# The recurrence of a hybrid encoder layer: its instructions recorded and issued by a list schedule in the kernel, with the branch products moved to other PSUM banks

## The chip, the cores and the metric

The kernel runs on one core of one Trainium2 chip. The metric is the device time of one execution in microseconds (us), the median of the runs shown. Engines are named as in the profile: PE (TensorE matmul), PEld (its weight load), DVE (VectorE), ACT (ScalarE), POOL (GpSimd), SP (the queue that issues most DMAs).

## The reference, cut to what matters

Sequence 512, model width 1024, two layers. Each layer projects the normalized input `h` and runs five mixers on it; their outputs are merged by gates:

```python
for l in range(DEPTH):
    p = jnp.einsum('bsd,dc->bsc', h, w_in[l])
    pa, pb, pc, pd, pm = split_last(p, mixer_sizes)
    o_a = mixer_dilated(pa, table_a)
    o_b = mixer_rwkv(pb, ...)          # a linear recurrence over 512 steps, both directions
    o_c = mixer_axial_gqa(pc, ...)
    o_d = mixer_diff(pd, ...)
    o_m = mixer_memory(pm, mem, w_mem_kv[l])
    y = gated_merge(h, (o_a, o_b, o_c, o_d, o_m), w_branch[l], w_gate[l], b_gate[l])
    out = jnp.einsum('bsd,de->bse', y, w_out[l])
    h = layer_norm(alpha * h + out, ln_g[l], ln_b[l])

# gated_merge, for each mixer i: sigmoid(h @ w_gate_i + b_i) * (o_i @ w_branch_i), summed
```

`mixer_rwkv` has 8 heads of 64; its step is `state = state * w + (state @ a) b^T + v k^T`, `y = state @ r`, run forward and backward and added.

## The kernel before

All activations lie transposed, 128 channels by 512 tokens. A float32 product is made of three matmuls on split operands (`gemm3_steps`, L145): hi*hi (L149), hi*lo (L150), lo*hi (L151), each 128x128 by 128x512. Weights come by DMA in chunks of 128x512 (`wraw`), ACT casts the high part (L135), DVE subtracts for the low part (L136).

Each layer has three stages. First the attention mixers (A, C, D, M). Then the recurrence (mixer B). Then the merge of mixer B (`branch_steps(1, ...)`), the product with `w_out` and the layer norm.

The recurrence works on 4 pairs of heads in 2 directions, 8 units. `early(p, e)` makes what a unit needs (projections `mixed` in the banks `pg`, low-rank products L826, exponentials, the products L907, L92, transposes L941 and L947). `late(p, e)` inverts the 32x32 triangles in 62 dependent DVE steps (L989, L991 on the tile `W`), combines them (L1007, L1014), then for two halves makes L1035, L1050 (read by DVE in L1053), L1061 and the four chained state steps L1068, each of which waits for the copies of the state `ST` on ACT (L1070) and DVE (L1071). `finish(p)` turns the sum of both directions, `SY`, back (L1092) and normalizes it. Many of these matmuls use a part of the array only (64x128, 64x64, 32x32).

The gates and branch products of mixers A, C, D and M (`fill`, L422) depend on nothing in the recurrence. For each of 8 column blocks `branch_steps` makes a gate product of 24 matmuls in a bank, ACT's tanh empties it (L406), then a branch product of 12 matmuls (6 for M), which DVE empties (L412 or L414, then adds to `y` in L416). In `fill` both products use the one bank `pf`:

```python
    ps = ps_f() if ch == "f" else ps_s()      # gate
    ...
    ps = ps_f() if ch == "f" else ps_g()      # branch
```

These are 1,104 matmuls a layer. The code weaves them in by `pull(1)`: after each `yield` of the recurrence one step (three matmuls) of `fill` is emitted; a few steps are pulled in the attention stage already (L649, L728). The final order on each engine is made by the framework's scheduler, which has its own durations; every engine then runs its queue in that order.

Of the kernel before, what the change touches and what calls it, by code (L numbers as in the profile page):

```python
# [13 lines left out]
AF = mybir.ActivationFunctionType  # L14
ALU = mybir.AluOpType
PSUM = bass.MemoryType.PSUM
# [32 lines left out]
NPAR = _off  # L49


@with_exitstack
def encoder_kernel(ctx: ExitStack, tc: tile.TileContext, x, mem, ln_in, rel_bias, w_in, par, w_up, a_up,
                   d_lambda, w_mem, w_branch, w_gate, w_out, lnp, cst, cossin, onehot, cnt, msk, out):
    nc = tc.nc

    const = ctx.enter_context(tc.tile_pool(name="const", bufs=1))
    big = ctx.enter_context(tc.tile_pool(name="big", bufs=1))
# [3 lines left out]
    def ps_g():  # L62
        return pp.tile([128, 512], F32, name="pg", tag="pg", bufs=2)

    def ps_f():
        return pp.tile([128, 512], F32, name="pf", tag="pf", bufs=1)
# [215 lines left out]
    with tc.tile_pool(name="init", bufs=1) as ip:  # L282
# [30 lines left out]
        for t in range(2):  # L313
            for j in range(2):
                ps = ps_s()
# [21 lines left out]
        for i in range(2):  # L337
            ps = ps_m()
# [11 lines left out]
    for l in range(L):  # L350
# [45 lines left out]
        def branch_steps(br, os, nk, done=None, ch="f", pool=wp, gb=1, order=None):  # L396
            k0 = K0[br]
            if os is None:
                os = reload(br, nk)
            for db in range(8):  # L400
                ps = ps_f() if ch == "f" else ps_s()
                w = split_w(w_gate[l, br * 8 + db], 1024, "f")
                yield from gemm3_steps(ps, [(*wk(w, k), hT[:, 0, k, :], hT[:, 1, k, :]) for k in range(8)])
                gt = pool.tile([128, S], F32, name="gt", tag="gt", bufs=gb)
                i = br * 8 + db
                act(gt, ps, AF.Tanh, scale=0.5, bias=hb[:, i:i + 1])  # L406
                ps = ps_f() if ch == "f" else ps_g()
                w = split_w(w_branch[l, db, :, k0 * 128:(k0 + nk) * 128], nk * 128, ch)
                yield from gemm3_steps(ps, [(*wk(w, k), o[:, 0, :], o[:, 1, :]) for k, o in zip(order or range(nk), os)])
                if y[db] is None:  # L410
                    y[db] = big.tile([128, S], F32, name="y", tag="y", bufs=8)
                    stt(y[db], gt, 1.0, ps, ALU.add, ALU.mult)  # L412
                else:
                    stt(gt, gt, 1.0, ps, ALU.add, ALU.mult)  # L414
                    if done is None:
                        tt(y[db], y[db], gt, ALU.add)  # L416
                    else:
                        tt(gt, y[db], gt, ALU.add)
                        done(db, gt)
# [10 lines left out]
        def pull(x):  # L430
            owed[0] += x
            while owed[0] >= 1:
                owed[0] -= 1
                next(fl, None)


        with tc.tile_pool(name=f"att{l}", bufs=1) as at:
# [115 lines left out]
            for hp in range(4):  # L553
# [4 lines left out]
                ps, ps2 = ps_g(), ps_g()  # L558
# [5 lines left out]
                k = k_stack(ps2)  # L564
                q = q_stack(ps)
                ps = ps_g()
# [3 lines left out]
                v = v_pair(vT, 4)  # L570
# [5 lines left out]
                for i in range(2):  # L576
                    b = load_bias(2 * hp + i)
                    p4 = []
                    for qb in range(4):
                        ps = ps_s()  # L580
                        score(ps, q, k, i, qb, S)
                        p, _ = softmax(ps, S, b[:, 384 - 128 * qb:896 - 128 * qb])
# [43 lines left out]
            ps = ps_g()  # L626
# [11 lines left out]
            for b in range(4):  # L638
                q = qn
                g = b // 2  # L640
                of = tile_of("oc", [128, S], F32, 2)
                for i in range(2):
                    p4 = []
                    for qb in range(4):
                        ps = ps_s()
                        score(ps, q, (kh, kl), i, qb, S, g)
                        p, _ = softmax(ps, S)
# [6 lines left out]
                t = gated(of, g2, True)  # L654
# [8 lines left out]
            with tc.tile_pool(name=f"attd{l}", bufs=1) as ad:  # L663
# [12 lines left out]
                for h in range(4):  # L676
                    ps = ps_g()
                    proj(ps, l, 48 + h, hT)
                    k = k_stack(ps)
                    ps = ps_g()  # L680
                    proj(ps, l, 44 + h, hT)
                    q = q_stack(ps)
                    ps = ps_g()
# [3 lines left out]
                    v = v_parts(vT, 4)  # L687
                    b = load_bias(8 + h)
                    p4 = []
                    for qb in range(4):  # L690
                        bs = b[:, 384 - 128 * qb:896 - 128 * qb]
                        ps, ps2 = ps_s(), ps_s()
# [21 lines left out]
            for b in range(2):  # L714
                k = k_stack(kvm[0][:, b, :], 256)
                v = v_pair(kvm[1][:, b, :], 2)
                ps = ps_g()
# [17 lines left out]
        with tc.tile_pool(name=f"rw{l}", bufs=1) as rp:  # L735
# [6 lines left out]
            def recurrence():  # L742
# [341 lines left out]
                def finish(p):  # L1084

                    q = pairs[p]
                    sy, bo = q["sy"], q["bo"]
                    po = ps_o()
                    for c in range(8):
                        for h in range(2):  # L1090
                            rw = slice(64 * (1 - h), 64 * (1 - h) + 64)
                            mm(po[64 * h:64 * h + 64, c * 64:(c + 1) * 64], sy[rw, c, :], ident[rw, rw], start=True, stop=True)  # L1092
                    ys = T("ys", [128, S])
                    nc.scalar.copy(ys, po)
                    yield
                    ps = ps_m()
                    mm(ps, ones_bd, ys, start=True, stop=True)
                    stt(ys, ps, -1.0 / 64, ys, ALU.mult, ALU.add)
                    sq = T("ysq", [128, S])
                    act(sq, ys, AF.Square)  # L1100
                    yield
                    ps = inv_norm(sq, ps_m(), ones_bd, 1.0 / 64, EPSG)
                    yield
                    tt(ys, ys, ps, ALU.mult)
                    ts(ys, ys, P("lng", p), P("lnb", p), ALU.mult, ALU.add)
                    tt(ys, ys, bo, ALU.add)
                    yield
                    g2 = silu2(rp, l, 16 + 14 + p, 1, "ysq")
                    stt(ys, ys, 0.5, g2, ALU.mult, ALU.mult)
                    if p == 3:  # L1110
                        oB.append(finish_o(rp, ys))
                        return
                    hi = rp.tile([128, S], F32R, name="yhi", tag="ysq", bufs=1)
                    nc.scalar.copy(hi, ys)
                    nc.sync.dma_start(out=scr_o[K0[1] + p, :, 0, :], in_=f(hi))
                    lo = ys.bitcast(F32R)
                    tt(lo, ys, f(hi), ALU.subtract)
                    nc.sync.dma_start(out=scr_o[K0[1] + p, :, 1, :], in_=ys)
                    yield

                pairs = {}
                units = [(p, e) for p in range(4) for e in range(2)]
                yield from early(*units[0])
                for n in range(len(units) + 1):
                    live = []
                    if n < len(units):
                        live.append(late(*units[n]))
                    if n and units[n - 1][1] == 1:
                        live.append(finish(units[n - 1][0]))
                    if n + 1 < len(units):  # L1130
                        live.append(early(*units[n + 1]))
                    while live:
                        for g in list(live):
                            if next(g, 0) == 0:
                                live.remove(g)
                            else:
                                yield

            for _ in recurrence():
                pull(1)  # L1140
            for _ in fl:
                pass


        with tc.tile_pool(name=f"out{l}", bufs=1) as op:
# [160 lines left out]
```

## Time and profile before

| | |
|---|---|
| median of 3 runs | 2253.56 us (2253.05 to 2254.36) |
| the profiled execution's own time | 2258.68 us |
| its span, first to last instruction | 2256.9 us |
| PE / PEld / DVE / ACT busy, share of the span | 97% / 75% / 77% / 56% |
| recurrence of layer 0 in the trace | about 515 to 1038 us |
| recurrence of layer 1 in the trace | about 1618 to 2139 us |

The median is 5.1 us below the profiled execution. Matmuls are pipelined and their ends are modelled in the profile, so the busy share of PE says less than the distance from one matmul's start to the next one's.

### The profile page before, as it was taken

Reading aid. Unit: us, or ns where it says so; the run is one execution under the profiler, and the core shown is the slowest. Engines: PE = TensorE matmul, PEld = TensorE weight load, DVE = VectorE, ACT = ScalarE, POOL = GpSimd, SP = SyncE. Lnnn points to the kernel's source line nnn. Section 1 sums busy time; section 2 is a strip of 40 time slices with the busy share of each in tenths; the row PEclk is TensorE's granted clock in tenths of the full one; section 3 lists DMA queues with packets and bytes.
Section 4 is the critical chain, followed back from the end, with each engine's and each line's share of the span. In section 5 each row is a group of like instructions: output and inputs, shape, how many; then the busy total and the mean of one; then the engine's idle time right before and its main releaser. Section 6 shows DMA issues by size and latency. Waiting matters only on the chain.

```text
span 2256.9 us, 36192 instructions
## 1 busy us (share of the span) xinstructions
PE 2191.7 (97%) x13040; PEld 1681.4 (75%) x13040; DVE 1727.2 (77%) x4228; ACT 1272.9 (56%) x2785; POOL 59.2 (3%) x117
## 2 busy tenths in 40 slices
PE   7999999999999999999999999999999999999998
PEld 6777777777777777777787777777777777777776
DVE  7777887677898797975567778766788979879565
ACT  4655666676555555544335656666665646565440
POOL 0000000100000000000000000001000000000000
PEclk9999999999999999999999999999999999999999
DMA  8732133322222321315333322333313213222251
GB/s 285 222 106 80 65 84 107 108 84 89 62 85 67 107 67 61 101 52 188 101 122 104 95 65 70 95 105 93 111 55 99 71 62 100 70 84 69 89 189 38
DMA packets 111780, 220.49 MB, mean 98 GB/s; under 512 B 13240, under 2 KB 23224, under 8 KB 111216
## 3 DMA queue, kind: packets, MB, share of 16 engines
q1 hardware_dynamic: 101456, 195.09, 27.0%
q0 software_dynamic: 10144, 23.08, 3.9%
q8 instruction: 103, 1.69, 0.3%
q14 instruction: 77, 0.63, 0.1%
HBM read 187.66 MB, written 27.31 MB: 95 GB/s over the span
## 4 chain that ended last, share of the span: by engine, by line
PE 72%; DVE 13%; ACT 8%; DMA 4%; issue 3%; SPq 0%; DVEq 0%; ACTq 0%
PE pg L150 10%; PE pg L151 10%; PE pg L149 10%; PE pf L149 6%; PE pf L150 5%; PE pf L151 5%; PE psc L470 4%; PE po L515 3%; PE pt L496 3%; DVE W L991 2%; DVE pr L989 2%; DMA wrawr<-in_w_out_dram 2%; DMA wrawr<-in_w_branch_dram 1%; DVE wlof L136 1%; PE po L505 1%
## 5 line engine op out<-in xcount | busy, mean ns | idle before, releaser
L150 PE MATMUL pg<-hT,whir 128*128 128x512 f32 (+1 forms) x912 | 366.0, 401 | 2.0 <-DVE hT L176 2.0
L149 PE MATMUL pg<-hT,whir 128*128 128x512 f32 (+1 forms) x912 | 364.5, 400 | 3.3 <-ACT whif L135 1.0
L151 PE MATMUL pg<-hT,wlor 128*128 128x512 f32 (+1 forms) x912 | 363.9, 399 | 0.9 <-DVE wlor L136 0.9
L136 DVE TENSOR_TENSOR wlor<-wrawr,whir 128x512 fp32r<-128x512 f32 x240 | 163.8, 687 | 116.0 <-ACT whir L135 105.7
L135 ACT CAST whir<-wrawr 128x512 fp32r<-128x512 f32 x240 | 147.7, 618 | 164.4 <-PE pg L150 113.2
L135 ACT CAST whif<-wrawf 128x512 fp32r<-128x512 f32 (+1 forms) x268 | 162.0, 605 | 126.3 <-PE pf L150 81.9
L149 PE MATMUL pf<-hT,whif 128*128 128x512 f32 x512 | 221.0, 432 | 3.4 <-DVE gt L414 2.9
L136 DVE TENSOR_TENSOR wlof<-wrawf,whif 128x512 fp32r<-128x512 f32 (+1 forms) x268 | 178.6, 668 | 43.1 <-ACT whif L135 37.9
L150 PE MATMUL pf<-hT,whif 128*128 128x512 f32 x512 | 206.7, 404 | 0.0
L151 PE MATMUL pf<-hT,wlof 128*128 128x512 f32 x512 | 205.0, 400 | 0.0
L149 PEld LDWEIGHTS pg<-hT,whir 128*128 128x128 f32 x912 | 172.4, 189 | 41.3 <-ACT whir L135 2.7
L150 PEld LDWEIGHTS pg<-hT,whir 128*128 128x128 f32 x912 | 172.4, 189 | 38.6 <-issue 3.1
L151 PEld LDWEIGHTS pg<-hT,wlor 128*128 128x128 f32 x912 | 172.6, 189 | 37.4 <-DVE wlor L136 3.4
L176 DVE TENSOR_TENSOR pT<-pt,pT 128x512 fp32r<-128x512 f32 x176 | 114.1, 686 | 35.7 <-ACT pT L175 34.6
L175 ACT CAST pT<-pt 128x512 fp32r<-128x512 f32 x176 | 94.6, 588 | 63.6 <-PE pt L496 63.1
L149 PEld LDWEIGHTS pf<-hT,whif 128*128 128x128 f32 x512 | 96.5, 188 | 35.7 <-DVE gt L414 10.3
L496 PE MATMUL pt<-cst,p 128*128 128x128 f32 x704 | 118.2, 273 | 0.0
L151 PEld LDWEIGHTS pf<-hT,wlof 128*128 128x128 f32 x512 | 96.4, 188 | 21.8 <-issue 1.6
L989 DVE TENSOR_TENSOR pr<-W,U 128x60 f32<-128x60 f32 (+24 forms) x496 | 103.3, 208 | 11.4
L991 DVE TENSOR_TENSOR W<-W,pr 128x60 f32<-128x60 f32 (+24 forms) x496 | 102.8, 207 | 11.1
L150 PEld LDWEIGHTS pf<-hT,whif 128*128 128x128 f32 x512 | 96.7, 189 | 19.1 <-issue 4.5
L496 PEld LDWEIGHTS pt<-cst,p 128*128 128x128 f32 x704 | 89.8, 141 | 27.7 <-DVE p L487 2.7
(330 smaller groups left out, 4803.8 us busy)
## 6 DMA issues: line engine op xcount, KB each, us to landing
wrawr<-in_w_in_dram SPq DMA_DIRECT2D x224, 256.0 KB, 2.8
wrawf<-in_w_gate_dram SPq DMA_DIRECT2D x160, 256.0 KB, 2.8
o<-scr_o POOLq DMA_DIRECT2D x26, 512.0 KB, 4.7
wrawf<-in_w_branch_dram SPq DMA_DIRECT2D x48, 256.0 KB, 2.7
bias<-scr_toe SPq DMA_DIRECT2D x24, 448.0 KB, 3.2
scr_o<-os SPq DMA_DIRECT2D x20, 512.0 KB, 2.9
wrawf<-in_w_in_dram SPq DMA_DIRECT2D x32, 256.0 KB, 2.8
wrawr<-in_w_out_dram SPq DMA_DIRECT2D x32, 256.0 KB, 3.1
```

The source lines that it names most:

```text
L135: nc.scalar.copy(hi, raw)
L136: tt(lo, raw, f(hi), ALU.subtract)
L149: mm(ps, ah, bh, start=(i == 0), stop=False)
L150: mm(ps, ah, bl, start=False, stop=False)
L151: mm(ps, al, bh, start=False, stop=(i == n - 1))
L175: nc.scalar.copy(hi, src)
L176: tt(lo, src, f(hi), ALU.subtract)
L470: mm(ps[:, :nk], q[:, i, sl], part[:, i if g is None else g, :nk], start=(j == 0), stop=(j == 1))
L496: nc.tensor.transpose(pt[:, qb * 128:(qb + 1) * 128], p4[qb][:, kb * 128:(kb + 1) * 128], ident)
L515: mm(po, vwin(kb), pT[:, b, :], start=(kb == 0 and b == 0), stop=(kb == nkb - 1 and b == 1))
L989: tt(pr, W[:, t8, s:s + 1].to_broadcast([128, nt, n]), U[:, s:s + 1, rsl].to_broadcast([128, nt, n]), ALU.mult)
L991: tt(W[:, t8, rsl], W[:, t8, rsl], pr, ALU.add)
```

## The change

A class `Conductor` stands between the kernel and the engines. From `record()` on, each engine call is kept with the tiles that it reads and writes, a cost and a rank. The whole rest of `fill` is recorded first, with rank 99; the recurrence then with the number of its unit (late, finish, early within it). `play()` makes a list schedule of both: at each step the engine that can start first takes, among the instructions whose inputs and buffers are ready, the one of the lowest rank (fill's matmuls come last, fill's work on other engines first), and consecutive small matmuls of one unit stay together as a group. The instructions are then issued in that order within `manual_schedule()`, so that each engine keeps it. While recording, a branch product takes a bank `pg`, of which there are two and which the recurrence's projections use as well. No instruction is added or left out.

```diff
+    def add(self, eng, op, real, a, k):
...
+        rank = self.rank
+        if rank[0] == 99 and eng != "tensor":
+            rank = (-1,)
...
+        o["group"] = o["i"]
+        if eng == "tensor":
+            p = self.last.get(self.rank)
+            if p is not None and p["eng"] == "tensor" and p["small"] and o["small"]:
+                o["group"] = p["group"]
...
+    def play(self):
...
+                    t = max(rt[g], s)
+                    o = groups[g][0]
+                    if 0 <= o["rank"][0] < 99 and o["rank"][0] > cur + self.ahead:
+                        continue
+                    pr = o["rank"] + (o["i"],)
+                    win = f0 + self.window(e, o)
...
+                    if t <= win:
+                        if now is None or pr < now[0]:
+                            now = (pr, max(t, f0), g)
+                    elif later is None or (max(t, f0), pr) < (later[1], later[0]):
+                        later = (pr, max(t, f0), g)
+                c = now or later
...
+        with self.tc.manual_schedule():
+            for o in order:
+                o["go"]()
+
+    run, ahead = 0, 1
...
-    nc = tc.nc
+    cd = nc = Conductor(tc)
...
-                ps = ps_f() if ch == "f" else ps_g()
+                ps = ps_f() if ch == "f" and cd.ops is None else ps_g()
...
-            for _ in recurrence():
-                pull(1)
+            cd.record()
+            cd.rank = (99, 0)
             for _ in fl:
                 pass
+            cd.rank = (0, 0)
+            recurrence()
+            cd.play()
```

In the changed kernel every recorded instruction has the line of the recorder (L122), every other one L67, so its rows are told apart by tiles.

PE, the middle of layer 0's recurrence, from a gate product (`pf<-hT`) to the branch product behind it (`pf<-o`); before:

```order
L151 MATMUL pf<-hT,wlof 128x512
L151 MATMUL pg<-hT,wlor 128x512
L149 MATMUL pg<-hT,whir 128x512
L150 MATMUL pg<-hT,whir 128x512
L151 MATMUL pg<-hT,wlor 128x512
L149 MATMUL pg<-hT,whir 128x512
L149 MATMUL pf<-o,whif 128x512
L150 MATMUL pf<-o,whif 128x512
```

The same hand-over in the changed kernel, near the end of layer 0's last unit, where `pt<-ST,PE` is a state step (L1068 of before):

```order
L122 MATMUL pf<-hT,whif 128x512
L122 MATMUL pt<-ST_5493,PE 128x128
L122 MATMUL pf<-hT,whif 128x512
L122 MATMUL pf<-hT,wlof 128x512
L122 MATMUL pt<-ST_5492,PE 128x128
L122 MATMUL pg<-o,whif 128x512 x2
L122 MATMUL pg<-o,wlof 128x512
```

Before, five matmuls of a projection stand between the last gate matmul and the first branch matmul in the same bank; now the branch product stands in another bank and follows one state step later.

PE, the end of layer 0's recurrence, from the last state step on (`po<-cst,SY` is the transpose in `finish` of the last pair); before:

```order
L1068 MATMUL pt<-ST_5131,PE 128x128
L1092 MATMUL po<-cst,SY 64x64
L149 MATMUL pf<-o,whif 128x512
L150 MATMUL pf<-o,whif 128x512
L151 MATMUL pf<-o,wlof 128x512
L149 MATMUL pf<-o,whif 128x512
L150 MATMUL pf<-o,whif 128x512
L151 MATMUL pf<-o,wlof 128x512
L1092 MATMUL po<-cst,SY 64x64 x15
```

The same place in the changed kernel:

```order
L122 MATMUL pg<-o,whif 128x512
L122 MATMUL po<-cst,SY 64x64 x16
L122 MATMUL pg<-o,whif 128x512
L122 MATMUL pg<-o,wlof 128x512
L122 MATMUL pg<-o,whif 128x512 x2
L122 MATMUL pm<-ys,cst 128x512
L122 MATMUL pg<-o,wlof 128x512
L122 MATMUL pf<-hT,whif 128x512 x2
```

Behind the last `po<-cst,SY` stand 30 of the 1,104 matmuls of fill before, and 281 now. Between the recurrence's first low-rank product and that point PE goes from a full-array matmul to a part-array block 97 times before and 80 times now, and back to fill and projection matmuls, from any of the recurrence's other matmuls, 176 times before and 142 times now. On DVE, 82 of fill's weight subtractions (L136) stand ahead of the recurrence's last `SY` before and 62 now, 22 and 14 of its L414, 27 and 14 of its additions to `y`.

## Rows read from the trace of the kernel before

**Rows 1.** The page, busy time by engine and granted TensorE clock in 40 slices

```profile
PE 2191.7 (97%) x13040; PEld 1681.4 (75%) x13040; DVE 1727.2 (77%) x4228; ACT 1272.9 (56%) x2785; POOL 59.2 (3%) x117
...
PEclk9999999999999999999999999999999999999999
```

**Rows 2.** Busy time by stretch: us, then PE, PEld, DVE, ACT, POOL, clock, DMA share, GB/s

```profile
515.00:1038.00 523.00, 507.29 (x3729) 379.54 (x3728) 427.88 (x1152) 299.54 (x709) 8.28 (x16) 0.99 0.24 76
1038.00:1133.00 95.00, 94.17 (x401) 73.73 (x400) 54.45 (x90) 33.05 (x57) 0.00 (x0) 1.00 0.49 158
...
1618.00:2139.00 521.00, 505.13 (x3730) 377.01 (x3729) 427.53 (x1151) 299.41 (x709) 8.32 (x16) 1.00 0.24 76
...
515.00:1020.00 505.00, 490.41 (x3639) 367.54 (x3637) 417.63 (x1135) 289.38 (x693) 7.20 (x14) 0.99 0.24 75
```

**Rows 3.** Groups by line, 515 to 1038 us: busy us, mean ns, idle before

```profile
L149 PE MATMUL pf<-hT,whif 128*128 128x512 f32 x229 | 99.7, 435 | 1.7 <-DVE gt L414 1.5
...
L136 DVE TENSOR_TENSOR wlof<-wrawf,whif 128x512 fp32r<-128x512 f32 (+1 forms) x88 | 57.8, 660 | 6.6 <-ACT whif L135 4.2 <-PE pf L151 2.2
...
L149 PE MATMUL pg<-hT,whir 128*128 128x512 f32 x128 | 51.7, 404 | 0.5 <-ACT whif L135 0.5
...
L149 PE MATMUL pf<-o,whif 128*128 128x512 f32 x100 | 45.9, 459 | 2.9 <-ACT gt L406 2.5
...
L414 DVE SCALAR_TENSOR_TENSOR gt<-gt,pf 128x512 f32<-128x512 f32 x24 | 16.4, 683 | 3.8 <-PE pf L151 3.5
```

**Rows 4.** PE in order of time, 695 to 700 us: start, duration, idle before

```profile
695.20 0.48 PE L150 MATMUL pg<-hT,whir 128*128 128x512 f32 x1
696.43 0.51 PE L149 MATMUL pf<-o,whif 128*128 128x512 f32 x1 [0.76 <-ACT gt L406]
...
697.01 0.39 PE L151 MATMUL pf<-o,wlof 128*128 128x512 f32 x1
697.24 0.39 PE L149 MATMUL pf<-o,whif 128*128 128x512 f32 x1
...
698.40 0.40 PE L151 MATMUL pf<-o,wlof 128*128 128x512 f32 x1
698.73 0.69 PE L92 MATMUL pm<-vsw,MB 128*64 128x64 f32 x16
699.35 0.50 PE L149 MATMUL pf<-o,whif 128*128 128x512 f32 x1
699.68 0.40 PE L150 MATMUL pf<-o,whif 128*128 128x512 f32 x1
```

**Rows 5.** The chain, 690 to 830 us: one block of each kind (start, us)

```profile
700.31 1.08 PE pm L907 x8
...
706.08 0.62 PE pt L1007 x30
...
709.84 0.89 PE pt L1035 x8
...
767.84 1.06 PE pt L1050 x16
...
803.96 1.08 PE po L1092 x32
...
807.32 0.86 PE pm L1097 x2
```

**Rows 6.** Who waited for whom, 515 to 1040 us: total, times, longest

```profile
PEld pt L1068 <- DVE ST L1071: 11.9, 29, 0.8
...
PEld pf L149 <- ACT gt L406: 7.8, 17, 1.1
...
PEld pf L149 <- DVE gt L414: 5.1, 12, 1.1
```

**Rows 7.** Busy time by stretches of 30 us, columns as in rows 2

```profile
545.00:575.00 30.00, 29.52 (x188) 23.04 (x187) 28.43 (x64) 22.24 (x58) 0.00 (x0) 1.00 0.13 39
...
995.00:1025.00 30.00, 29.48 (x292) 21.89 (x291) 12.90 (x30) 10.80 (x28) 0.00 (x0) 1.00 0.17 51
```

More of the change, by code (lines that the diff above doesn't have):

```diff
@@ L1122, in recurrence @@
                 units = [(p, e) for p in range(4) for e in range(2)]
-                yield from early(*units[0])
+                cd.rank = (0, 2)
+                for _ in early(*units[0]):
+                    pass
                 for n in range(len(units) + 1):
@@ L1126, in recurrence @@
                     if n < len(units):
-                        live.append(late(*units[n]))
+                        live.append(((n, 0), late(*units[n])))
                     if n and units[n - 1][1] == 1:
-                        live.append(finish(units[n - 1][0]))
+                        live.append(((n, 1), finish(units[n - 1][0])))
                     if n + 1 < len(units):
-                        live.append(early(*units[n + 1]))
+                        live.append(((n, 2), early(*units[n + 1])))
                     while live:
[L1133 to L1137, printed above, removed]
-            for _ in recurrence():
-                pull(1)
+                        for rg in list(live):
+                            cd.rank = rg[0]
+                            if next(rg[1], 0) == 0:
+                                live.remove(rg)
+            cd.record()
+            cd.rank = (99, 0)
             for _ in fl:
                 pass
+            cd.rank = (0, 0)
+            recurrence()
+            cd.play()
         with tc.tile_pool(name=f"out{l}", bufs=1) as op:
```

274 lines of the change are left out of this document (added).

## The prediction

> **What bounds the kernel now.** I read the page first, then a table of busy time by stage, then the recurrence stage by groups, in order of time, by its chain and by its waits.
>
> The page puts PE at 97% busy and its clock at the full level, 2.4 GHz, in every slice [rows 1]. That share alone proves little, since a matmul's shown end is modelled. So look at starts: inside a product the 128x512 matmuls start 0.23 us apart, while each is shown as 0.39 to 0.40 us long [rows 4]. PE therefore loses time wherever two starts lie further apart, and most such losses don't show as idle time.
>
> The stage table gives the recurrence 523 us in layer 0 and 521 in layer 1, 46% of the span [rows 2]. The merge stage behind it has 401 matmuls in 95 us, 0.24 us each: there PE is full, and no order of instructions can help. So I price the recurrence, layer 0, and double it.
>
> Its PE work, by starts: fill has 3 x 229 gate and 3 x 100 branch matmuls in the window, the projections 3 x 128 [rows 3], the low-rank products 32 by the code; 1,403 matmuls by 0.232 us (between the 0.23 and 0.24 that stand in rows 4) are 326 us. The small blocks, by the chain [rows 5]: 16 of L1035 at 0.89, 16 of L1050 and 16 of L1061 at 1.06, 16 of L907 (both banks together) at 1.08, 16 of L92 at 0.62 (start to next start, rows 4), 16 of L1007 and L1014 at 0.62, 4 of L1092 at 1.08; 56 state steps and 112 transposes at two records or one by 0.11 (L1035's 0.89 for 8 records); 16 full-width float32 products at 0.86. Together 128 us. Changing over costs too: a full matmul ahead of a part-array block takes 0.33 us to the next start instead of 0.23, and the first one behind it again 0.33 [rows 4]. With 97 entries and 176 returns in the order, that is 27 us. Sum 481 of 523. **About 42 us a layer are waits.**
>
> Who is waited for? The hand-over inside fill is one: the branch product can't start before ACT has emptied the bank of the gate product, and the next gate not before DVE has emptied the branch product. In one case PE's starts lie 1.23 us apart, 1.0 more than normal [rows 4]. PEld waits 7.8 us for the one and 5.1 for the other [rows 6]. The rest, some 30 us, are the recurrence's own results coming late, mostly state copies and sums on DVE; PEld's wait for the state copy, 11.9 us, is the largest of them [rows 6].
>
> DVE is the second limit: 417.6 us busy in the 505 us up to the recurrence's end, 83% [rows 2], up to 95% in its fullest stretch, but only 43% in the last one, where fill and the last state steps are alone [rows 7].
>
> **The change, part by part.**
>
> *Work.* No instruction comes or goes: 0 us from work as such. What can change is changing over, waiting, and what lies beside what.
>
> *Banks.* The branch product goes to another bank, so the tanh of the gate runs beside 6 or 12 matmuls, and the emptying of the branch product beside the next gate's 24. It removes at least the 4.0 us of PE's own idle time at these places (1.5 and 2.5 in rows 3), at most PEld's 12.9 [rows 6]. I take 10, nearer to PEld's figure, because in the case of rows 4 PE lost 1.0 us where its own idle time says 0.76. The cover for the new place is the second `pg` bank; when projections hold both, the old wait returns, at about 1 us each. The Trainium skill speaks against this term: its page "TensorE: Matmul & The Clock Gate", section "HAM oscillation", tells of a thin matmul kernel in which double-buffering PSUM gave nothing further. By that the term would be 0 and the sum 2230 us. This trace does not agree: it has waits on these very banks, 12.9 us a layer of PEld's time [rows 6].
>
> *Groups.* The order has 17 fewer entries and 34 fewer returns; at 0.10 us each that is 5 us. Lower bound 3 (the returns alone), upper 8 (if blocks that now follow each other save an exit as well).
>
> *Priority.* This is the largest move. Fill's matmuls come last in rank, so 281 of them stand behind the recurrence's last transpose, where 30 stood before. These 251 matmuls, 58 us by 0.232, leave the recurrence and make a stretch of fill alone. On PE that is neutral: the same work later, at full pace, since 36 matmuls (8.3 us) need only three weight chunks. It is neutral only if the recurrence then really ends that much earlier.
>
> *Waits.* Of the other 30 us the new order can take all or none, or it can add some: an engine that keeps a fixed order stops everything behind an instruction whose input is late. With PE, what is queued behind is fill that could have run; DVE then waits for that PE work in turn. I can't price this from a row of before. I take 7 us, a quarter. Not more, because DVE gets less slack: 20 subtractions (0.66 us), 8 of L414 and 13 additions (0.68 each [rows 3]) leave the recurrence, 27 us (the additions by L414's mean), so DVE has 390 us of work left in what would be 505 - 58 - 22 = 425 us, 92% instead of 83%.
>
> *Tail.* `finish` of the last pair, with its table loads and waits, now lies beside 281 matmuls; I count its few us in the term above. The weights of the merge stage are loaded in that stretch as well, but PE is full in the merge stage already [rows 2]: 0.
>
> *Other stages.* Fewer fill matmuls are done ahead of the recurrence (115 against 150 by the first low-rank product, by the order); that is work moved on a full engine, 0.
>
> **Sum.** 10 + 5 + 7 = 22 us a layer, 44 us in both. From the profiled execution's 2258.7 that gives 2214.7; the median of the runs lies 5.1 lower, so I forecast **2210 us** for the median (-2.0%). With the bounds of the first two terms (7 to 21 a layer) and 0 to 15 for the waits it is 2182 to 2239: the forecast's own range, rounded to 2185 to 2238.
>
> **Rivals.**
>
> *A. The schedule holds almost perfectly.* All waits go: 10 + 5 + 30 = 45 a layer, 2164 us. For it: full-width matmuls repeat at 0.23 us and DVE's groups have steady means, so a good table of durations can plan closely. Against it: DVE would then have to be 97% busy for 400 us, and its fullest 30 us reach 95% [rows 7].
>
> *B. DVE becomes the bound (the other side).* If DVE can't be held above the share that it has now, the recurrence needs 390 / 0.83 = 470 us instead of 425; then 58 us of fill follow, in which DVE has little to do. That is 528 against 505, 23 us worse a layer, 2300 us. It decides at 447 us, where DVE is 87% busy: above that the change gains, below it loses. For it: 95% was seen for 30 us and 83% as the mean. Against it: independent DVE work can start as soon as its rank allows, and fill's matmuls no longer stand ahead of the recurrence on PE. At 85%, the middle, it is 2277. The Trainium skill's page "Perfetto Trace Analysis", section "Optimization Strategy", advises to interleave stretches that load different engines; here fill, which loads PE, is partly taken out of the stretch that loads DVE, and by that rule the time would go this way.
>
> *C. Only the bank counts.* The new order waits as much as the old: 10 us a layer and nothing else, 2234 us; it lies in the forecast's range. If the second bank is held by projections as well, the gain falls to nothing, 2254: no change.
>
> **Chances.** Forecast, 2185 to 2238: 0.56. A, below 2185: 0.12. Between 2238 and 2249, the bank's gain partly eaten: 0.07. Within 0.2% of before (2249 to 2258; this kernel's three runs spread over 0.06%, and 0.2% is about what a measurement can tell from no change): 0.08. B, slower: 0.17. So faster 0.75, same 0.08, slower 0.17. The range 2165 to 2262 leaves out the low end of A and most of B, some 0.2.
>
> **What the profile would show.** In the changed kernel: no idle time of PE at the first `pg<-o` matmul of a branch product with ACT's tanh as releaser; the last `SY` some 65 us before the end of fill, and ahead of 950 us in layer 0; behind it full matmuls 0.23 us apart; DVE above 87% up to that point; fewer starts of 0.33 us. I would be wrong if DVE's share stays at 83% and the last `SY` comes after 962 us (rival B), if PE's waits for DVE's copies grow, if SP's weight loads come late, because `wraw` has two buffers a kind and fill's loads stand in one queue with the recurrence's, or if PE's clock falls in the recurrence.

## The result and the profile after

The changed kernel takes **2358.55 us** (median of 4 runs, 2353.94 to 2365.79) against 2253.31 us before: ratio **1.047, interval 1.0443 to 1.0497**. It is 105 us slower where 44 us faster was forecast. The profiled execution has 2353.94 us.

The page of the changed kernel, busy time and granted clock as in [rows 1]:

```profile
PE 2190.3 (93%) x13040; PEld 1673.6 (71%) x13040; DVE 1721.4 (73%) x4228; ACT 1276.0 (54%) x2785; POOL 59.1 (3%) x117
...
PEclk9999999989799999999999999999989999999999
```

The instruction counts are those of [rows 1], and the busy time of PE, DVE, ACT and POOL is within 6 us of what it was (PEld's within 8); only the span grew. So the loss is waiting or worse overlap. The clock, which had no dip in the page's slices, now falls at the start of each layer's recurrence, where PE has its holes.

Where does the time go? The four pairs of a layer can be cut at the transposes of `SY` that end each (this recorded code has one line, so the view of the tile `po` finds them):

```profile
L122 PE MATMUL po<-cst,SY x32: 311/311/366, 704.2 to 705.9; 64*64 64x64 f32 x32
...
L122 PE MATMUL po<-cst,SY x32: 218/218/267, 803.9 to 804.8; 64*64 64x64 f32 x32
...
L122 PE MATMUL po<-cst,SY x32: 218/218/267, 906.5 to 907.4; 64*64 64x64 f32 x32
...
L122 PE MATMUL po<-cst,SY x32: 218/218/267, 1011.6 to 1012.6; 64*64 64x64 f32 x32
```

With these cuts, stretches of layer 0 of the changed kernel, from attention's last transpose (507 us) to fill's end, in the columns of [rows 2]:

```profile
507.00:704.00 197.00, 154.97 (x1059) 114.73 (x1059) 147.10 (x379) 104.25 (x244) 3.43 (x7) 0.90 0.22 66
704.00:1012.00 308.00, 290.37 (x2417) 212.55 (x2418) 252.68 (x731) 176.08 (x431) 2.15 (x4) 0.99 0.22 67
1012.00:1084.00 72.00, 69.06 (x311) 53.31 (x308) 35.70 (x60) 29.94 (x51) 1.61 (x3) 1.00 0.55 176
```

and the same of the kernel before:

```profile
505.00:676.00 171.00, 166.30 (x1123) 125.78 (x1124) 143.13 (x386) 101.53 (x239) 3.43 (x7) 0.98 0.25 80
676.00:1020.00 344.00, 334.11 (x2567) 249.63 (x2561) 279.87 (x758) 191.91 (x462) 3.77 (x7) 1.00 0.24 75
1020.00:1035.00 15.00, 13.88 (x80) 9.78 (x79) 7.54 (x13) 7.71 (x11) 0.15 (x1) 1.00 0.21 65
```

Read the first number behind each window. **Start** (up to the first `SY`): 171 became 197 us, +26. **Pairs** (the other three): 344 became 308, -36. **Tail** (fill alone): 15 became 72, +57. The sum is +47 us; layer 1 gives 168, 344, 15 before and 196, 308, 71 after, +48. Both together are the 95 us between the two profiled executions. The table below uses these three stretches for every kernel.

The same rows say what kind of time it is. A stretch less PE's busy time is PE's idle time: in the start it grew from 5 to 42 us, in the pairs from 10 to 18, in the tail from 1 to 3. Together that is the +47. And the counts of PE's matmuls say where fill went: the pairs have 150 fewer (2417 against 2567), which at the prediction's 0.232 us are 35 us, and they are 36 us shorter. The start has 64 fewer, 15 us, and is 26 us longer. (Counted by fill's own tiles it is 166 fewer in the pairs, 61 in the start, and 247 more in the tail.) So the pairs paid back what left them; **the start didn't**.

The start has three big holes. PE of the changed kernel in order of time, the instructions around them:

```profile
508.10 1.10 PE L67 MATMUL po<-pT,v 128*128 128x512 f32 x3 [0.23 <-DVE pT L67]
516.36 1.22 PE L122 MATMUL pg<-o,whif 128*128 128x512 f32 x2 [7.16 <-ACT whif L122]
...
585.73 0.40 PE L122 MATMUL pf<-hT,wlof 128*128 128x512 f32 x1
594.90 0.76 PE L122 MATMUL psc<-AR,BK 64*128 64x128 f32 x2 [8.78 <-DVE pr L122]
...
694.00 0.63 PE L122 MATMUL pf<-hT,whif 128*128 128x512 f32 x2
703.47 0.79 PE L122 MATMUL pg<-hT,whir 128*128 128x512 f32 x1 [8.83 <-ACT whir L122]
```

25 us of idle time in three places; in the kernel before no hole between 505 and 705 us reaches 1.3 us. The first one's releaser is a weight split on ACT; here is ACT at that time:

```profile
511.31 0.62 ACT L67 CAST os<-of 128x512 fp32r<-128x512 f32 x1 [1.49 <-DVE of L67]
515.38 0.40 ACT L122 CAST W<-msk 128x256 f32<-128x256 bf16 x1 [3.45 <-DMA scr_o<-os]
515.70 0.61 ACT L122 CAST whif<-wrawf 128x512 fp32r<-128x512 f32 x1
```

ACT's first recorded instruction is the copy into `W`, needed much later. The schedule counts W's SBUF as free, but it waits for a spill of attention's `os`; the fixed order keeps every weight split behind it, and PE behind those. Behind the third hole stands a load:

```profile
702.27 0.62 ACT L122 CAST uphi<-tmp 128x512 fp32r<-128x512 f32 x1 [9.08 <-DMA tmp<-in_a_up_dram]
702.80 1.13 ACT L122 CAST whir<-wrawr 128x512 fp32r<-128x512 f32 x2
```

ACT stood 9.08 us for a weight of the low-rank products, and the weight split that PE waited for was queued behind that.

### The profile page after: what moved, and what is told of

The parts are those of the page before. It is cut to its first block, busy times and chain, and to the rows that moved or that the text cites. A ratio compares the mean times of both kernels' runs of the same rounds, so it can differ in the third digit from the quotient of the medians.

```text
span 2352.2 us, 36223 instructions
## 1 busy us (share of the span) xinstructions
PE 2190.3 (93%) x13040; PEld 1673.6 (71%) x13040; DVE 1721.4 (73%) x4228; ACT 1276.0 (54%) x2785; POOL 59.1 (3%) x117
## 5 line engine op out<-in xcount | busy, mean ns | idle before, releaser
L67 PE MATMUL pg<-hT,whir 128*128 128x512 f32 (+1 forms) x1248 | 416.5, 402 | 4.8 <-DVE hT L67 2.0
L122 PE MATMUL pf<-hT,whif 128*128 128x512 f32 x948 | 322.7, 409 | 7.9 <-ACT gt L122 7.4
L67 PEld LDWEIGHTS pg<-hT,whir 128*128 128x128 f32 x1248 | 233.2, 190 | 55.0 <-ACT whir L67 4.1
L67 PE MATMUL pg<-hT,wlor 128*128 128x512 f32 (+1 forms) x624 | 249.7, 400 | 0.9 <-DVE wlor L67 0.9
L122 PE MATMUL pg<-hT,whir 128*128 128x512 f32 x576 | 193.9, 412 | 25.1 <-ACT whir L122 21.4
L122 PEld LDWEIGHTS pf<-hT,whif 128*128 128x128 f32 x948 | 175.1, 189 | 54.0 <-ACT gt L122 12.3
L122 PE MATMUL pf<-hT,wlof 128*128 128x512 f32 x474 | 191.9, 405 | 0.4 <-DVE wlof L122 0.4
L122 ACT CAST whif<-wrawf 128x512 fp32r<-128x512 f32 (+1 forms) x176 | 105.3, 598 | 126.4 <-PE pf L122 67.0
L67 DVE TENSOR_TENSOR wlor<-wrawr,whir 128x512 fp32r<-128x512 f32 x168 | 114.5, 686 | 64.9 <-ACT whir L67 54.3
L122 DVE TENSOR_TENSOR wlof<-wrawf,whif 128x512 fp32r<-128x512 f32 (+1 forms) x176 | 116.5, 662 | 59.2 <-ACT whif L122 56.8
L122 PE MATMUL pg<-o,whif 128*128 128x512 f32 x416 | 144.6, 415 | 15.0 <-ACT whif L122 15.0
L67 ACT CAST whir<-wrawr 128x512 fp32r<-128x512 f32 x168 | 103.1, 619 | 92.7 <-PE pg L67 60.7
L122 PEld LDWEIGHTS pg<-hT,whir 128*128 128x128 f32 x576 | 107.4, 191 | 59.6 <-ACT whir L122 26.4
L67 DVE TENSOR_TENSOR pT<-pt,pT 128x512 fp32r<-128x512 f32 x176 | 114.0, 685 | 40.3 <-ACT pT L67 39.2
L67 PEld LDWEIGHTS pg<-hT,wlor 128*128 128x128 f32 x624 | 119.0, 191 | 25.0 <-DVE wlor L67 3.0
L67 ACT CAST pT<-pt 128x512 fp32r<-128x512 f32 x176 | 94.6, 588 | 65.9 <-PE pt L67 65.5
L67 PE MATMUL pt<-cst,p 128*128 128x128 f32 x704 | 120.3, 277 | 4.2 <-ACT p L67 2.9
L67 ACT ACTIVATE p<-p,sst 128x512 f32<-128x512 f32 (+1 forms) x160 | 110.8, 699 | 17.2 <-DVE sst L67 16.1
L122 PE MATMUL pg<-hT,wlor 128*128 128x512 f32 x288 | 117.1, 407 | 0.7 <-DVE wlor L122 0.7
L67 PEld LDWEIGHTS pt<-cst,p 128*128 128x128 f32 x704 | 90.5, 142 | 32.6 <-ACT p L67 4.5
L122 DVE TENSOR_TENSOR W<-W,pr 128x60 f32<-128x60 f32 (+24 forms) x496 | 102.7, 207 | 9.6
L122 DVE TENSOR_TENSOR pr<-W,U 128x60 f32<-128x60 f32 (+24 forms) x496 | 102.2, 206 | 8.7
```

Source lines behind the costliest of these rows:

```text
L67: return real(*a, **k)
L122: o = dict(i=len(self.ops), eng=eng, op=op, go=lambda: real(*a, **k), rank=rank, preds={}, tiles=[])
```

## The experiments

All ratios are against runs of the kernel before on the same chip. Layer 0 in us, cut as above; "att." is the end of attention, where a kernel moved it.

| kernel | median us | ratio (interval) | start | pairs 2, 3, 4 | tail |
|---|---|---|---|---|---|
| before | 2253 to 2256 | 1 | 171 | 128, 128, 88 | 15 |
| changed | 2358.6 | 1.047 (1.0443-1.0497) | 197 | 100, 103, 105 | 72 |
| e1 bank alone | 2360.7 | 1.0461 (1.0445-1.0477) | 189 | 139, 144, 92 | 15 |
| e2 changed, no bank | 2433.0 | 1.0775 (1.0747-1.0803) | 183 | 97, 107, 104 | 128 |
| e3 changed, free order | 2292.2 | 1.017 (1.014-1.02) | 168 | 105, 101, 99 | 72 |
| e4 changed, spread rank | 2288.8 | 1.0139 (1.0122-1.0156) | 194 | 112, 130, 100 | 6 |
| e5 before, banks divided (att. +11) | 2299.3 | 1.02 (1.0185-1.0215) | 181 | 118, 132, 91 | 15 |
| e6 changed, banks divided (att. +11) | 2310.4 | 1.0251 (1.0228-1.0275) | 201 | 101, 115, 98 | 33 |
| e7 changed, later SBUF | 2323.0 | 1.0308 (1.0288-1.0329) | 177 | 102, 102, 105 | 74 |
| e8 spread, free order | **2245.3** | **0.9961 (0.9947-0.9975)** | 174 | 114, 128, 98 | 6 |
| e9 as e8, later SBUF | 2246.9 | 0.9967 (0.9955-0.998) | 173 | 113, 128, 99 | 6 |
| e10 as e8, no bank | 2265.5 | 1.005 (1.0034-1.0065) | 169 | 108, 136, 103 | 18 |
| e11 as e4, later SBUF | 2271.3 | 1.0071 (1.0054-1.0088) | 185 | 113, 129, 102 | 6 |
| e12 as e11, other prices | 2302.6 | 1.0212 (1.0192-1.0232) | 184 | 122, 127, 103 | 6 |
| e13 fixed on PE, DVE | 2345.7 | 1.0405 (1.0389-1.042) | 193 | 103, 103, 105 | 71 |
| e14 fixed on ACT, SP | 2337.6 | 1.0368 (1.035-1.0385) | 188 | 106, 101, 101 | 74 |
| e15 changed, late recording | 2320.1 | 1.0294 (1.0278-1.0311) | 176 | 101, 102, 106 | 73 |
| e16 as e15, spread | 2271.5 | 1.0075 (1.0059-1.009) | 184 | 112, 128, 100 | 6 |
| e17 as e7, less fill | 2132.3 | single run | 177 | 94, 94, 93 | - |

Theory 1: the fixed order costs, because one late input holds up a whole engine. Theory 2: the rank costs, because fill ranked last leaves a tail that the recurrence doesn't pay back. The rival to both, from the first run on: the bank costs.

**e1, the bank alone**, in the kernel before:

```
-                ps = ps_f() if ch == "f" else ps_g()
+                ps = ps_f() if ch == "f" and not rec[0] else ps_g()
...
+            rec[0] = True
             for _ in recurrence():
                 pull(1)
```

> The kernel before with one part of the change: in the recurrence stage the branch product takes a bank of pg, the order stays the framework's. My prediction's bank term (10 us a layer) expects 2230 to 2240 us. If the hand-over was covered by other waits, as the page on the clock gate has it for its kernel, 2249 to 2258. If the projections of the recurrence hold both banks of pg and fill then waits for them (rival: the new bank costs more than the old one), over 2262.

Measured 2360.65 us: +104, as much as the whole change, and against the sign of my term. PE of e1 around the second pair's first projection (`whir`):

```profile
608.90 0.40 PE L150 MATMUL pg<-o,whif 128*128 128x512 f32 x1
...
610.38 0.51 PE L151 MATMUL pg<-o,wlof 128*128 128x512 f32 x1
610.73 0.40 PE L149 MATMUL pg<-hT,whir 128*128 128x512 f32 x1
```

and in the kernel before:

```profile
568.57 0.39 PE L151 MATMUL pf<-hT,wlof 128*128 128x512 f32 x1
568.80 0.40 PE L150 MATMUL pg<-hT,whir 128*128 128x512 f32 x1
```

In e1 three branch products (576 to 611 us) go through `pg` ahead of this projection, which starts 42 us later than before. Each waits for a gate product, and `pf` takes one of those at a time. So the recurrence's next pair stands behind fill.

**e5, the two banks divided**, in the kernel before; outside the recurrence `pg0` and `pg1` are taken in turn:

```
+        return pp.tile([128, 512], F32, name="pg", tag="pg%d" % (0 if rec[0] else turn[0]), bufs=1)
+    def ps_b():
+        return pp.tile([128, 512], F32, name="pb", tag="pg1", bufs=1)
...
-                ps = ps_f() if ch == "f" else ps_g()
+                ps = (ps_b() if rec[0] else ps_f()) if ch == "f" else ps_g()
```

> The kernel before, order left to the framework, and pg's two banks divided in the recurrence: one for the projections, the other for fill's branch products alone. Contention theory (in e1 the branch product's place in the rotation of pg's two banks makes fill and the projections wait for each other, 104 us): with the banks apart most of it goes, 2245 to 2285 us; a single bank for the projections may cost a little. If a second bank for fill is bad for another reason (fill running ahead and taking PE or ACT from the recurrence), it stays above 2320.

2299.26 us: 61 of the 104 come back, though taking turns in attention costs 11 us in layer 0 before the recurrence begins. The projection is back at its place, 573.8 us:

```profile
573.32 0.39 PE L156 MATMUL pb<-o,whif 128*128 128x512 f32 x1
573.55 0.39 PE L157 MATMUL pb<-o,whif 128*128 128x512 f32 x1
573.78 0.39 PE L156 MATMUL pg<-hT,whir 128*128 128x512 f32 x1
```

So most of e1's loss is the sharing, not the second bank itself; of the 43 us left, attention's turns are a part, and the rest isn't placed.

**e2, the bank undone inside the schedule** (the condition on `cd.ops` taken out of that line).

> The changed kernel with the bank edit undone: fill's gate and branch products share pf again, the list schedule is made anew with that. If the bank helps inside the schedule as my prediction has it, 2375 to 2400 us (10 to 20 us a layer worse than 2359). If the branch product's competition with the projections for pg is what stalls PE (the 8.9 us hole at 586 us), below 2345.

2432.98 us, 74 worse: the first answer's direction and more than its size. With one bank and the lowest rank, fill gets on less: the pairs hold 416 of its matmuls against 530 and are as long (308 us), and the tail grows to 128 us. The same edit costs in one order and pays in another.

**e6, the banks divided in the schedule** (as e5).

> The changed kernel with the same division: one bank of pg for the recurrence's projections, the other for the branch products, planned anew. Its plan leaves 110 matmuls behind the last SY instead of 283 and has no hole at the place of the 8.9 us one. If the contention for pg makes a good part of the loss in the schedule too, 2290 to 2325 us; if the loss is all from the fixed order and the rank, 2345 to 2370.

2310.40 us. Contention is part of the loss: the tail falls from 72 to 33 us, and the hole at 586 us is gone (the longest behind the start is 2.2 us). The start now holds 328 of fill's matmuls, by tiles, where the changed kernel's has 200, and is 4 us longer (201 us). So fill's low rank alone doesn't keep it out of the start; the shared banks do their part. Attention's 11 us are in the 2310.

**e3, the planned order left to the framework's scheduler:**

```
-        with self.tc.manual_schedule():
-            for o in order:
-                o["go"]()
+        for o in order:
+            o["go"]()
```

> The changed kernel, recorded and planned the same way, but the planned order is handed to the framework's scheduler, which may move instructions again on each engine. Theory 1 (a fixed order on each engine makes PE stand behind late inputs: the plan runs 90 us a layer ahead of the chip) expects most of the loss back, 2250 to 2290 us. Theory 2 (fill has the lowest rank, so it is left over as a tail whoever orders) expects 2330 to 2370.

2292.23 us; 66 of the 105 come back, and the table says where: the start falls from 197 to 168, pairs 308 to 305, the tail stays at 72. Its stretches:

```profile
507.00:675.00 168.00, 150.50 (x1025) 113.97 (x1023) 140.91 (x366) 100.30 (x236) 3.46 (x7) 0.93 0.20 63
675.00:980.00 305.00, 292.81 (x2406) 217.72 (x2405) 257.29 (x739) 176.48 (x432) 2.16 (x4) 0.99 0.23 71
980.00:1052.00 72.00, 69.52 (x317) 54.01 (x316) 36.16 (x62) 30.21 (x51) 1.82 (x3) 1.00 0.55 176
```

Behind the start, the fixed order is within 3 us of the framework's. The hole at 586 us isn't the fixed order's: here it stands at 580 us, 8.2 us long. Against the kernel before, the pairs are 39 us shorter with 166 of fill's matmuls fewer (39 us), and the start 3 us shorter with 81 fewer (19 us). What e3 still loses lies in the start, where PE is idle for 17.5 us (168 less 150.50) and was for 4.7.

**e4, fill ranked last in its unit, not behind all units** (`spread` is called where the kernel before pulled):

```
+                def spread(n):
+                    cd.rank = (n, 3)
+                    next(fl, None)
...
                             if next(rg[1], 0) == 0:
                                 live.remove(rg)
+                            else:
+                                spread(n)
```

> The changed kernel with fill's rank changed alone: each step of fill is recorded between the recurrence's steps as before and ranks last inside its unit, not behind all units; the list schedule and the fixed order stay. By the plan 18 matmuls stand behind the last SY instead of 283. Theory 2 (the rank, thus the tail, costs the 49 us a layer) expects 2250 to 2290 us. Theory 1 (the fixed order costs it, tail or not) expects the last SY to come later by what the tail gets shorter, 2330 to 2370.

2288.83 us, 70 back. The tail goes (72 to 6); pairs grow by 34 (308 to 342), about what their 165 more matmuls of fill take (38 us). The gain is in the start again: it takes 105 more (24 us) and is 3 us shorter, and the hole at 586 us is gone. So both theories hold, but not as separate shares: the three removals from the changed kernel give back 66 (e3), 70 (e4) and 48 us (e6), together more than the 105.

**e8, both together.**

> The changed kernel with fill's rank inside the units (as e4) and the order left to the framework (as e3). If rank and fixed order are two separate losses (66 and 70 us), they add up to 2220 to 2235 us. If they are the same loss taken away twice, 2280 to 2300. What is left above 2256 then is the bank's.

2245.33 us, between the two answers: 113 us better than the changed kernel, five sixths of the sum of the two gains (136), and 0.4% faster than before:

```profile
505.00:679.00 174.00, 166.78 (x1129) 127.34 (x1128) 145.56 (x386) 104.19 (x245) 3.45 (x7) 0.99 0.26 81
679.00:1019.00 340.00, 332.09 (x2572) 249.69 (x2570) 282.94 (x764) 189.96 (x458) 3.77 (x7) 1.00 0.24 75
1019.00:1025.00 6.00, 6.00 (x50) 4.42 (x50) 1.79 (x3) 2.24 (x5) 0.47 (x1) 1.00 0.12 44
```

**e10, e8 without the bank.**

> e8 with the bank edit undone (gate and branch products share pf). If the branch product's place among the projections' banks costs time in any order that the framework makes (in e1 104 us), this is the fastest, 2190 to 2235 us. If the list schedule needs the second bank (undoing it in the changed kernel cost 75 us), 2270 to 2320. If the plan's order and the bank only matter together, 2240 to 2256.

2265.52 us, outside all three answers: here the bank is worth 20.2 us, 10.1 a layer. Who waited for whom in e10, PEld from 515 to 1040 us:

```profile
PEld pf L122 <- ACT gt L122: 12.4, 16, 1.5
PEld pf L122 <- DVE gt L122: 7.2, 9, 1.5
```

In e8 the first is 0.3 us and the second isn't there (`pg`, which the branch products use there, waits 1.2 us for DVE's `gt`). The list order without the bank is 0.5% slower than before.

**e7, SBUF of the recurrence planned as free 10 us later:**

```
-            t = tags.setdefault(s["tag"], dict(free=[0.0] * s["bufs"]))
+            t = tags.setdefault(s["tag"], dict(free=[10000.0 if "_rw" in s["tag"] else 0.0] * s["bufs"]))
```

> The changed kernel whose plan counts the recurrence's SBUF tiles as free 10 us after its start, so that ACT's first instruction is a weight split and no longer the copy into W, which stood 3.5 us for attention's last spill with everything behind it. If the start is the whole of theory 1 (the 7.4 us hole and what it moves), 2335 to 2348 us; if the late start is only caught up later, 2354 to 2364.

2323.00 us, better than either answer. ACT's recorded instructions in e7:

```profile
495.31 0.62 ACT L122 CAST whir<-wrawr 128x512 fp32r<-128x512 f32 x1
...
508.79 0.64 ACT L122 CAST whir<-wrawr 128x512 fp32r<-128x512 f32 x1
516.58 0.41 ACT L122 CAST W<-msk 128x256 f32<-128x256 bf16 x1 [3.47 <-DMA scr_o<-os]
```

The copy into `W` waits as long as before, but five other recorded instructions now go ahead of it, into attention's end. Of the 20 us that the start gains, 2 are the first hole (7.4 to 5.3 us by PE's starts) and 7 the third one (9.0 to 2.2), so later holes move with the start; the hole at 586 us stays (8.6).

**e9, e8 with e7's start.**

> e8 (rank inside the units, order left to the framework) with e7's start (the recurrence's SBUF tiles planned from 10 us). If the framework's scheduler already moves the copy into W out of the way, the start is worth nothing more: 2240 to 2250 us like e8's 2245. If the plan's order still weighs at the start, 2225 to 2238.

2246.94 us: nothing more. A scheduler that may move the copy doesn't need the hint.

**e11, e4 with e7's start.**

> e4 (rank inside the units, fixed order on each engine) with e7's start. If the fixed order costs only through the start hole, this comes down to e8's 2245 us (2240 to 2252). If the fixed order also stands in the way later, by jitter that the plan doesn't know, 2258 to 2280.

2271.29 us. The fixed order still costs 24 us against e9, and again at the start: 185 against 173; the pairs have 344 and 340.

**e12, e11 with the trace's prices for small matmuls:**

```
-                o["pitch"] = 1.7 * n * r * c / 16384
+                o["pitch"] = 39 if c == 32 else 67 if n <= 128 and min(r, c) == 64 else 1.7 * n * r * c / 16384
```

> e11 with the schedule's prices of the small matmuls set to what the trace shows: 39 ns for each 32x32x32 (planned at 3), 67 for those with 64 rows or columns (planned at 27 to 109). In the changed kernel 18 of the 82 us by which PE falls behind the plan are such prices. If prices are what makes the plan run ahead, 8 to 20 us faster than e11. If the order hardly depends on them, within 6 us of e11.

2302.64 us, 31 slower: both answers missed. In the profiled executions, 21 us apart, the loss lies in each layer's second pair (122 against 113 us, and 125 against 112). Nor are the new prices nearer everywhere. A block of L907 is 8 matmuls, half of them in each of two banks, and takes 1.08 us [rows 5], 135 ns each: the old price was 109, the new one is 67. So the run doesn't test better prices, and why this list is worse stays open.

**e13 and e14, the order fixed on half of the engines:** `manual_schedule(engines={...})` with PE and DVE, or with ACT and SP.

> The changed kernel with the planned order kept on PE and DVE alone; ACT, SP and POOL are left to the framework. If the fixed order costs through what stands first in ACT's and SP's queues (the copy into W, the weight loads), most of the 66 us come back, 2290 to 2310 us. If PE's or DVE's own order is what stands behind late inputs, 2335 to 2360.

> The counterpart: the planned order is kept on ACT and SP alone; PE, DVE and POOL are left to the framework. If ACT's and SP's queues carry the cost, 2335 to 2360 us; if PE's or DVE's order does, 2290 to 2310. In both halves some 2325 would say that each carries a part.

2345.67 and 2337.62 us: each time the answer that blames the half which stays fixed. So neither half is free of the cost, and freeing one gives back little: either one, held fixed, keeps most of the loss (53 and 45 of 66 us).

**e15 and e16, recording begins behind the low-rank products' projections** (`cd.record()` and the recording of fill moved into `recurrence`, ahead of `early` of the first unit).

> The changed kernel, recording begins only behind the low-rank products' projections: these are left to the framework and may mingle with attention's end. If the fixed order costs at the start alone (in e3 the whole gain of 29 us a layer lies before the first SY; the later pairs take as long), 2285 to 2310 us. If it costs in every pair, 2335 to 2358.

> e15 with fill's rank inside the units (as e4), the order fixed on every engine from there on. If the start and the rank are the two losses, it comes to e8's time, 2240 to 2256 us, although the order is fixed. If the framework's freedom is needed all along, 2262 to 2290 (e11 had 2271).

2320.11 and 2271.47 us. e15 gets 38 of the 66 us, all at the start (176); e16 is where e11 was, against its first answer. What remains of the fixed order's cost with spread rank (10 to 12 us a layer at the start) I can't place further.

**e17, less fill.** This kernel leaves out the gate and branch products of mixers C, D and M, so its result isn't the layer's.

> e7 with fill cut short: the gate and branch products of mixers C, D and M are left out (the merge lacks their terms), so that from the second pair on next to no fill stands beside the recurrence. It asks how long a pair takes by itself; with fill ranked last a pair took 102 to 105 us, with fill beside it as before 128. Rival B of the prediction (DVE's chain paces the recurrence, it can't get much shorter) expects 92 to 105 us a pair, with DVE busy less than before. If the fill that is still beside it holds the pairs up through PE's queue, 70 to 82 us; the plan gives 75.

With no fill beside them the pairs take 94, 94 and 93 us:

```profile
684.00:965.00 281.00, 214.70 (x1922) 155.28 (x1918) 218.15 (x677) 144.86 (x377) 1.64 (x3) 0.79 0.12 38
```

DVE is busy 78% of it (218.15 of 281) and PE 76%, so neither is full; that fits a chain that hops between DVE, PE and ACT. PE's clock was 0.79 here, and what a pair would take at the full clock isn't measured; but from the second pair to the third it fell from 0.85 to 0.79, and both took 94 us. Nor is 94 us a floor for every pair: the last pair of the kernel before takes 88 us, at the full clock and with 192 matmuls of fill in it.

## Why the prediction was wrong, step by step

*Priority*, which I put at 0, is the first step that failed: "neutral only if the recurrence then really ends that much earlier". The tail grew by 57 us, as said (72 us against my 65). The three pairs gave back their part: 36 us for the 35 us of matmuls that left them. The start, up to the first `SY`, gave next to nothing back. With a free order (e3) it lost 19 us of fill's matmuls and became 3 us shorter; PE stood idle instead, 17.5 us against 4.7. I had priced the recurrence as one stretch in which PE is full, and the start isn't once fill is taken out: it is 168 us long with 180 of fill's matmuls (e3) and 174 with 283 (e8). Given back inside the units, the rank is worth 47 us (e3 to e8) or 70 (changed to e4).

Rival B had the sign, and e3, which has the rank without the fixed order, comes near its time (2292 us against 2300); I gave it 0.17. The changed kernel is 59 us above it, so B isn't the whole. B's reason was a share that DVE couldn't exceed. The share stays where it was: in the pairs 81% before (279.87 of 344), 82% after, 84% in e3, 83% in e8; in the start 84% before, in e3 and in e8 (75% in the changed kernel, with its holes). But that it is the cause isn't shown: no run changed DVE's work alone, and in e17's pairs DVE is at 78% and the pairs still take some 94 us. The Trainium skill's page "Perfetto Trace Analysis", section "Optimization Strategy", on interleaving stretches that load different engines, which I cited beside rival B, agrees with e3 and e8: the more evenly interleaved e8 is 47 us faster.

*Waits*, -7 us a layer, failed in sign. The fixed order costs 29 us at the start (197 against e3's 168) and 3 in the pairs. I had named the danger ("stops everything behind an instruction whose input is late") and looked for it in the recurrence; some 20 of the 29 us come back when only the beginning of the recorded order is changed (e7, e15). That is the seam to attention, for which my sum had *Other stages: 0*. PEld's waits in the changed kernel, 515 to 1040 us, to be set beside [rows 6]:

```profile
PEld pg L122 <- ACT whir L122: 13.4, 5, 9.3
PEld pt L122 <- DVE ST L122: 13.3, 23, 1.3
...
PEld pg L122 <- ACT whif L122: 8.5, 2, 7.5
...
PEld pf L122 <- ACT gt L122: 4.7, 4, 1.8
```

The state copy's wait is nearly as it was (11.9 to 13.3 us); new are the weight splits, `whif` at the start (7.5 us) and `whir` at 703 us (9.3).

*Banks*, -10 us a layer, has the right size where the order lets it work: 10.1 a layer (e10 to e8), with the very waits gone that it was costed from. That 10 meets 10.1 is partly luck: e10, whose order is another, has 19.6 us of these waits where the kernel before had 12.9. The Trainium skill's "TensorE: Matmul & The Clock Gate", section "HAM oscillation", told of no gain from double-buffered PSUM in its kernel; e8 and e10 differ from that by 20.2 us. But I priced the case that "projections hold both" at "about 1 us each". In e1 the projections stood behind fill instead, 42 us late, and the edit alone cost 52 us a layer. In the changed kernel the hole at 586 us is of this kind: e6, with the banks divided, doesn't have it (nor has e4, where fill ranks higher).

*Groups*, -5 us, and the forecast of fewer 0.33 us starts I didn't measure apart. *Work*, 0, was right.

What the profile should have shown: no wait of the branch product for the tanh (right; its 7.8 us of idle time are the weight split); the last `SY` some 65 us ahead of fill's end (right, 72) and before 950 us (wrong, 1012); DVE above 87% (wrong, 80% from 515 to 1012 us: 396.42 us of 497, below); of the signs of error, the last `SY` came after 962 us with DVE's share no higher, a load came late (ACT's 9.08 us), and PE's clock fell (0.90 in the start).

```profile
515.00:1012.00 497.00, 443.75 (x3471) 326.61 (x3473) 396.42 (x1105) 278.31 (x671) 5.58 (x11) 0.96 0.22 67
```

One way from the changed kernel back to the one before: fixed order 66 (changed to e3), rank 47 (e3 to e8), less the 9 that e8 has over before, 104 us. These are differences along one path and must add up to the whole; by another path the rank is 70 and the order 44 (e4 to e8), and the banks' part lies inside both.

## What to carry to other kernels

Filler ranked behind everything moves its work to the end; what it leaves is saved only in the stretches that the filler's engine bounds. Here the later pairs paid back what left them, and the first stretch paid back next to nothing. So price such a move stretch by stretch, by the idle time that the engine would have there, and not by the stage's average. An order fixed on every engine has to be right about the state in which it begins: plan the buffers and queues that the stage before still holds, or leave the seam to a scheduler. A second buffer helps only if those who share it don't then queue for each other: look at what is handed out next to it.

## What the runs showed of the hardware

How far order alone moves the time: every engine of the changed kernel is busy as long as before within 8 us, and yet the kernels of one and the same work (all but e17) span 2245 to 2433 us. The granted clock was lower where PE had longer holes (1.00 is 2.4 GHz): 0.98 in the start before, where none reached 1.3 us, 0.90 with three of 7 to 9 us, and 0.79 in e17's pairs, with holes of up to 11.9 us. Other prices for a greedy schedule's small matmuls moved the time by 31 us (e12) for a reason that stays open, so one schedule's time says little of its rules.
